# Cached keys fetched page by page, score products at full height, and grouped products in a one-layer decoder kernel

## The chip, the cores and the metric

The kernel runs on one core of a Trainium2 chip. The metric is device time in microseconds (us) of one execution; the median of several runs is compared. Within a core five engines work from in-order queues of their own: PE (matrix products), DVE (vector), ACT (scalar functions and copies), POOL (which here mostly issues gathers) and SP (which here issues loads). An instruction that waits holds up everything behind it in its queue.

## The reference

One decoder layer is applied with the same weights to 512 prompt tokens and to 8 sample rows of 4 tokens each. The parts that the change touches belong to the sample rows' sparse attention and to the norms:

```python
def dsa_sample(q, k_new, v_new, qi, ki_new, wi, ck, cv, cki, page_table):
    ...
    ki_past = cki[page_table].reshape(DB, PAST_LEN, IDX_DIM)
    ki_all = jnp.concatenate([ki_past, ki_new], axis=1)
    sc = index_scores(qi, wi, ki_all)
    ...
    _, idx = lax.top_k(sc, topk)
    ...
    k_sel = jnp.where(is_new, k_new[bi, new_idx], ck[phys, off])
    v_sel = jnp.where(is_new, v_new[bi, new_idx], cv[phys, off])
    return sparse_attend(q, k_sel, v_sel, valid)
```

Each sample row has 2048 cached tokens in 16 pages of 128 tokens, found through a page table; index keys, keys and values each lie in a paged cache. The best 256 of 2052 tokens by index score take part in a softmax attention. The prompt has the same attention over its own 512 tokens. Then come a gMLP mix, the output projection, an attention to a 256-token memory, a product-key expert layer of 16384 experts with the best 16 of each of 8 heads, and norms (mean of squares over 1024 features) before each of these.

## The kernel before

**Main stream.** Every large projection is the function `mm3`: a float32 product is made of three products of rounded halves (lines 249, 250 and 251). `wtile` loads a weight tile of 512 KB by SP (line 225), ACT casts it to the upper half (line 213) and DVE subtracts to get the lower half (line 217, called the split below). The raw tile and both halves have two buffers each, so the load of tile k waits for the split of tile k-2, and the cast of tile k waits for the products of tile k-2. I count the main products in order of program: w_in takes numbers 1 to 912, the memory keys and values (wKV, tiles K1 to K8) 913 to 1104, then for the first half of the prompt eight tiles of the output projection (wO1 to wO8) and four of the memory queries (wMQ1 to wMQ4) up to 1392; behind 1392 comes the second half (h1), with its own eight wO tiles, later the experts.

**Work beside it.** Generators run between the main products:

- The mask search for the prompt: a search by bits for each token's threshold score, in which ACT counts (line 695, two activations a bit, 32 bits) and DVE decides (lines 698, 705, 692). Lines 706 to 727 finish it, and the prompt's attention (lines 854 to 890: scores 854, softmax 860 to 867, transposes 880, values 886) follows.
- The sample rows: index scores (`sample_scores`, products at line 1359, a batch for each of 8 rows), the select (`sample_select`, 32 bits on DVE, line 1413 first in each bit, lines 1426 to 1453 behind the last), scores of the cached keys (`sample_keys`, line 1496, evacuated at line 1500), and the attention proper (`sample_attend`: lines 1562 and 1535 spread the selection, 1545 and 1546 turn the weights, 1553 is the product with the values, a round for each row, 1601 to 1638 close it).
- The norms: `squares4` sums squares on PE with four small products (line 147) in four column groups.

**What sets the order.** The program is recorded through a scheduler that plans all engines on a timeline of its own and writes each engine's queue in that order; pools of few buffers and the generators' yields shape it. So an edit can move instructions that it does not touch.

**Fetches.** Pages of index keys (32 KB) are fetched by SP (line 1317 reads a page number, line 1319 issues the transfer), 8 behind each weight load. Cached keys and values are gathered by POOL (line 1276), four gathers of 128 pieces for each sample row, into a ring of three buffers (`RING`) which keys use first and values after them.

Of the kernel before, what the change touches and what calls it, by code (L numbers as in the profile page):

```python
# [10 lines left out]
I32 = mybir.dt.int32  # L11
U32 = mybir.dt.uint32
AF = mybir.ActivationFunctionType
ALU = mybir.AluOpType
AX = mybir.AxisListType
# [3 lines left out]
P = 128  # L19
NP = 512  # L20
NS = 32
NT = NP + NS
KT = 8
# [28 lines left out]
class Kernel:  # L52
# [84 lines left out]


    def squares4(self, room, x, kt, st, w):
        sq = self.t(room, [P, w], tag="nsqs", bufs=4)  # L140
        self.nc.scalar.square(sq, x)
        self.sq4 = [sq] if kt % 4 == 0 else self.sq4 + [sq]
        if kt % 4 == 3:
            n = w // len(st)
            for i, ps in enumerate(st):
                for c, q in enumerate(self.sq4):
                    self.nc.tensor.matmul(ps[c * NS : c * NS + NS, :n], self.ones[:, :NS], q[:, i * n : i * n + n],
                                          start=kt == 3, stop=kt == KT - 1, skip_group_check=True)

# [69 lines left out]
    def wtile(self, pool, src, kt=KT, n=P):  # L219

        more = pool is self.pw and self.gp is not None and self.RX
        if more:
            self.raws = (self.raws + 1) % (2 + self.RX)
        raw = self.t(self.gp, [P, kt, n], tag="wraw", bufs=self.RX) if more and self.raws > 1 else self.t(pool, [P, kt, n], tag="wraw", bufs=2)
        load = self.nc.sync.dma_start(raw, src)  # L225
        self.loads += 1
        if self.todo and self.loads > 2:
            self.index_rows(load)
        hi = self.t(pool, [P, kt, n], F32R, tag="whi", bufs=2)
        lo = self.t(pool, [P, kt, n], F32R, tag="wlo", bufs=2)  # L230
        self.split(hi, lo, raw)
        return hi, lo
# [399 lines left out]
    def masks(self, pool, room, qiT, kiT, wi_n, mb):  # L632
        nc = self.nc
        scs = []
        for b in range(1, 4):
# [4 lines left out]
            for h in range(8):  # L640
                if h % 2 == 0:

                    pair = [self.pst("pb") for _ in range(2)]
                    for o, ps in zip((0, 64), pair):
                        nc.tensor.matmul(ps[:, :L], qiT[o : o + 64, h // 2, ts], kiT[o : o + 64, :L], start=True, stop=True)
                ps = pair[h % 2]
# [198 lines left out]
    def attend(self, pw, qT, kT, v_n, mb):  # L845
# [24 lines left out]
        def values(b, r, sms):  # L870
# [11 lines left out]
            if r % 2:  # L882

                for s in range(b + 1):
                    for g in range(2):
                        nc.tensor.matmul(yb[g * 64 : g * 64 + 64, (r - 1) * P : (r + 1) * P], v_n[:, s, g * 64 : g * 64 + 64],
                                         keep[g][:, s, :, :], start=s == 0, stop=s == b, skip_group_check=True)
            if r == 3:
# [372 lines left out]
    def fetch_kv(self, s2):  # L1261
        n = len(self.kv)
        if n < 16:
            kv = self.t(s2, [P, 2048], tag="kv", bufs=self.RING)
            kv = kv.rearrange("p (m x) -> p m x", m=4)
            for m in range(4):
                self.gather(kv[:, m, :], self.I["cV" if n >= 8 else "cK"], self.s_ix[:, n * 4 + m : n * 4 + m + 1])
            self.kv.append(kv)

    RING = 3  # L1270
# [8 lines left out]
    def pages(self, s1, s2):  # L1279
# [3 lines left out]
        for r in range(0, P, 32):  # L1283
            nc.gpsimd.iota(pid[r : r + 32], [[0, 1]], base=0, channel_multiplier=1, allow_small_or_imprecise_dtypes=True)
        pt_i = self.t(s1, [P, P], I32)
        nc.gpsimd.dma_start(pt_i, I["page_table"].rearrange("b n -> (b n)").partition_broadcast(P))
        pf = self.t(s1, [P, P])
        nc.vector.tensor_copy(pf, pt_i)
        self.s_ix = self.t(s1, [P, 64], I32)
        tmp = self.t(s1, [P, 64])  # L1290
        for u in range(4):
            r = slice(u * 32, u * 32 + 32)

            nc.vector.tensor_scalar(tmp[r, :32].rearrange("p (b c f) -> p b c f", c=2, f=2),
                                    pf[r].rearrange("p (b c v r f) -> p v r b c f", c=2, v=2, r=2, f=2)[:, u % 2, u // 2],
                                    32.0, pid[r], ALU.mult, ALU.add)
            nc.vector.tensor_scalar(tmp[r, 32:], pf[r].rearrange("p (n u) -> p u n", u=4)[:, u], 32.0, pid[r], ALU.mult, ALU.add)
        nc.vector.tensor_copy(self.s_ix, tmp)

        self.kv, self.rows, self.indexed, self.keyed = [], [], False, False  # L1300
        for b in range(8):
            if b % 2 == 0:
                kx = self.t(s1, [P, 4, 512], tag="S8", bufs=2) if b < 4 else self.t(s2, [P, 2048], tag="kv", bufs=self.RING).rearrange("p (b x) -> p b x", b=4)
            self.rows.append(kx[:, b % 2 * 2 : b % 2 * 2 + 2, :].rearrange("p b (m x) -> p (b m) x", x=P))
        self.todo, self.loads = [(pt_i, b, m) for b in range(8) for m in range(8)], 0
        for _ in range(self.RING - 2):
            self.fetch_kv(s2)


    def index_rows(self, behind):  # L1310
        nc = self.nc
        src = self.I["cI"].rearrange("(n d) x -> n d x", d=64)
        with self.tc.issue_after(getattr(behind, "ins", behind)):
            for pt_i, b, m in self.todo[: self.PAGES]:
                for c in range(2):
                    n = b * 16 + 2 * m + c
                    page = nc.values_load(pt_i[:1, n : n + 1], engines=[mybir.EngineType.SP], min_val=0, max_val=src.shape[0] - 1,
                                          skip_runtime_bounds_check_because="a page table holds pages of the pool")
                    nc.sync.dma_start(self.rows[b][c * 64 : c * 64 + 64, m, :], src[bass.ds(page, 1)].rearrange("n d x -> (n d) x"))
        self.todo = self.todo[self.PAGES :]  # L1320

    PAGES = 4


    def sample_scores(self, s1, s2):
# [26 lines left out]
        for b in range(8):  # L1352
            kx = self.rows[b]
            while any(x[1] == b for x in self.todo):
                yield 1.0
# [101 lines left out]
    def sample_keys(self, s1, s2):  # L1457
# [8 lines left out]

        qs = self.t(s2, [P, 4, 8, 16])
        self.s_room = Room(qs.rearrange("p e b q -> p (e b q)"))
        ps = self.pst("pb")
        for e in range(4):  # L1470
            perm = self.t(s1, [P, P], tag="qst", bufs=2)
            nc.vector.tensor_copy(perm.rearrange("p (u g d) -> p u g d", u=4, g=2),
                                  self.ident.rearrange("p (g e d) -> p e g d", g=2, e=4)[:, e].unsqueeze(1).to_broadcast([P, 4, 2, 16]))
            nc.tensor.matmul(ps[:, e * P : e * P + P], perm, self.s_q.rearrange("p r t -> p (r t)"), start=True, stop=True)
        for e in range(4):
            nc.scalar.activation(qs[:, e].rearrange("p b (r t) -> p r b t", r=4), ps[:, e * P : e * P + P].rearrange("p (r b t) -> p r b t", r=4, b=8),
                                 AF.Copy, scale=0.125)

        own = self.t(s2, [P, 4])
        nc.vector.tensor_reduce(own, self.ident.rearrange("p (r c d) -> p c r d", r=2, d=16), AX.XY, ALU.add)  # L1480
        yield 1.0
# [4 lines left out]
        for b in range(8):  # L1486
            q4 = self.t(s2, [P, 4, 64], tag="q4", bufs=2)
            nc.vector.tensor_tensor(q4.rearrange("p e (c q) -> p e c q", c=4), qs[:, :, b].unsqueeze(2).to_broadcast([P, 4, 4, 16]),
                                    own.unsqueeze(1).unsqueeze(3).to_broadcast([P, 4, 4, 16]), ALU.mult)

            pair = [self.pst("pb") for _ in range(2)]
            for e in range(4):
                for f in range(2):
                    for o, ps in zip((0, 64), pair):
                        for c in range(2):
                            nc.tensor.matmul(ps[c * 64 : c * 64 + 64, f * P : f * P + P], q4[o : o + 64, e],
                                             self.kv[b][o : o + 64, 2 * c + f, e * P : e * P + P], start=e == 0 and f == 0, stop=e == 3,
                                             skip_group_check=True, tile_position=(o, c * 64))
            for r, ps in enumerate(pair):
                nc.scalar.copy(self.s_S[b].rearrange("p (m r f x) -> p r f m x", m=4, r=2, f=2)[:, r],  # L1500
                               ps[:, : 2 * P].rearrange("p (f m x) -> p f m x", f=2, m=4))
            self.fetch_kv(s2)
            yield 4.0 * self.SK
        self.keyed = True

    SK = 1.0

    def sample_attend(self, s2, s1):
# [40 lines left out]
        def values(b, A):  # L1549
            po = self.pst("pb")  # L1550
            for m in range(4):
                for c in range(4):
                    nc.tensor.matmul(po[c * NS : c * NS + NS, :P], A[:, m, c, :], self.kv[8 + b][:, c, m * P : m * P + P],  # L1553
                                     start=m == 0, stop=m == 3)
            nc.scalar.copy(part(b), po[:, :P])
            self.fetch_kv(s2)
# [314 lines left out]
```

## Time and profile before

| | |
|---|---|
| median of 3 runs | 1797.67 us (1795.82 to 1801.38) |
| the profiled execution, its own time | 1793.41 us |
| its span in the trace | 1791.7 us |
| PE busy | 1675.7 us, 94% |
| DVE busy | 1482.9 us, 83% |
| ACT busy | 863.2 us, 48% |
| POOL busy | 503.6 us, 28% |
| main products (lines 249 to 251), busy | 2515 us of overlapping records, 2544 of each line |
| DMA | 460.36 MB, mean 257 GB/s |

Busy time is what the records of an engine cover; matrix products overlap in PE's pipeline, so the sum over a line can be larger than the engine's busy time. The profiled execution lies 4.3 us below the median of the runs.

### The profile page before, as it was taken

How to read it: one execution, taken by the hardware profiler on the slowest of the kernel's cores; microseconds unless marked ns; L12 is line 12 of the kernel's file. 1: busy time of each engine (PE TensorE's matmuls, PEld its weight loads, DVE VectorE, ACT ScalarE, POOL GpSimd, SP SyncE). 2: the span in 40 equal slices, each digit the busy share in tenths (PEclk: the TensorE clock that was granted, in tenths of full speed). 3: DMA queues.
4: the chain of work that ended last, by engine and by line, in shares of the span. 5: the costliest groups of instructions: out<-in, count | busy, mean ns of one | idle time of the engine just before them, and what ended most of it. 6: DMA issues, size and time to landing. Idle time of an engine off the chain costs nothing. (4 is left out here: it accounts for less than half of the span.)

```text
span 1791.7 us, 30106 instructions
## 1 busy us (share of the span) xinstructions
PE 1675.7 (94%) x10494; PEld 1476.6 (82%) x10494; DVE 1482.9 (83%) x3654; ACT 863.2 (48%) x1584; POOL 503.6 (28%) x437
## 2 busy tenths in 40 slices
PE   7999889989996999799999999999999999999995
PEld 5879757778875889789899998888788888888884
DVE  4586899755759999998999887799898888878897
ACT  4355765764543434674675575233343333333333
POOL 3000123120000054223224222334333534345343
PEclk9999769989998999999999999999999999999997
DMA  5423425445752599789779789799998999999986
GB/s 179 128 83 98 126 85 199 140 166 170 238 172 90 169 345 329 267 316 334 256 269 322 242 306 316 267 353 333 360 356 300 375 357 328 349 334 324 358 305 231
DMA packets 195207, 460.36 MB, mean 257 GB/s; under 512 B 17976, under 2 KB 98616, under 8 KB 193648
## 3 DMA queue, kind: packets, MB, share of 16 engines
q1 hardware_dynamic: 132928, 241.63, 39.7%
q0 software_dynamic: 53072, 207.71, 32.5%
q10 hardware_dynamic: 9056, 9.11, 1.6%
q8 instruction: 82, 1.34, 0.3%
q14 instruction: 69, 0.57, 0.1%
HBM read 416.11 MB, written 42.05 MB: 256 GB/s over the span
## 5 line engine op out<-in xcount | busy, mean ns | idle before, releaser
L251 PE MATMUL t<-t,t 128*128 128x384 f32 (+3 forms) x2544 | 867.9, 346 | 12.5 <-DVE t L217 12.2
L250 PE MATMUL t<-t,t 128*128 128x384 f32 (+3 forms) x2544 | 867.6, 343 | 0.0
L249 PE MATMUL t<-t,t 128*128 128x384 f32 (+3 forms) x2544 | 779.9, 346 | 17.6 <-ACT t L213 15.1
L213 ACT CAST t<-t 128x1024 fp32r<-128x1024 f32 (+4 forms) x512 | 418.2, 841 | 716.8 <-PE t L250 475.8
L217 DVE TENSOR_TENSOR t<-t,t 128x1024 fp32r<-128x1024 f32 (+4 forms) x512 | 488.6, 965 | 140.0 <-ACT t L213 136.3
L251 PEld LDWEIGHTS t<-t,t 128*128 128x128 f32 x2544 | 485.0, 191 | 66.4 <-DVE t L217 15.7
L249 PEld LDWEIGHTS t<-t,t 128*128 128x128 f32 x2544 | 485.0, 191 | 61.2 <-ACT t L213 20.3
L250 PEld LDWEIGHTS t<-t,t 128*128 128x128 f32 x2544 | 485.4, 191 | 38.4 <-issue 5.7
L1276 POOL DMA_INDIRECT t<-in_u,t x160 | 201.7, 1260 | 499.0 <-DVE t L1736 305.0
L1276 POOL DMA_INDIRECT t<-in_v,t x160 | 215.5, 1347 | 298.0 <-DVE t L1741 233.9
L1741 DVE SCALAR_TENSOR_TENSOR t<-t,t,t 128x1024 f32<-128x1024 f32 x160 | 204.9, 1281 | 4.5 <-DMA t<-in_v,t 3.6
L1736 DVE SCALAR_TENSOR_TENSOR t<-t,t 128x1024 f32<-128x1024 f32 x160 | 193.8, 1219 | 8.7 <-DMA t<-in_u,t 8.6
L1081 ACT ACTIVATE t<-t 128x512 f32<-128x512 f32 x96 | 96.6, 1148 | 19.3 <-DMA wd<-t 18.5
L1276 POOL DMA_INDIRECT t<-in_cK,t x32 | 32.3, 1009 | 212.1 <-PE t L1359 146.5
L1217 DVE TENSOR_TENSOR t<-t,t 128x352 f32<-128x352 f32 x128 | 66.6, 521 | 6.2 <-DMA t<-wd 4.0
L1097 ACT ACTIVATE t<-t 128x384 f32<-128x384 f32 x128 | 62.3, 487 | 11.8 <-PE t L251 9.2
L1071 ACT ACTIVATE t<-t,t 128x128 f16<-128x128 f16 x192 | 58.2, 395 | 10.1 <-DVE t L1067 7.4
L1078 PE MATMUL t<-t,t 128*128 128x128 f16 x384 | 51.8, 221 | 9.4 <-ACT t L1081 8.8
L1276 POOL DMA_INDIRECT t<-in_cV,t x32 | 34.2, 1069 | 72.0 <-PE t L1553 45.1
L695 ACT ACTIVATE t<-t,t 128x384 f32<-128x384 f32 x64 | 42.7, 666 | 24.4 <-DVE t L692 20.3
L1079 PE MATMUL t<-t,t 128*128 128x128 f16 x384 | 49.7, 221 | 0.4 <-DVE t L1073 0.3
L1079 PEld LDWEIGHTS <-t 128*128 128x128 f16 x384 | 36.7, 98 | 10.6 <-issue 10.1
(400 smaller groups left out, 1471.2 us busy)
## 6 DMA issues: line engine op xcount, KB each, us to landing
t<-in_uT SPq DMA_DIRECT2D x128, 512.0 KB, 5.8
t<-in_v SPq DMA_DIRECT2D x128, 512.0 KB, 6.2
wd<-t POOLq DMA_DIRECT2D x11, 2048.0 KB, 9.2
t<-wd SPq DMA_DIRECT2D x32, 704.0 KB, 7.9
gd<-t SPq DMA_DIRECT2D x56, 192.0 KB, 5.3
t<-gd SPq DMA_DIRECT2D x56, 192.0 KB, 7.6
t<-in_wA SPq DMA_DIRECT2D x19, 512.0 KB, 4.0
t<-in_wO SPq DMA_DIRECT2D x16, 512.0 KB, 4.0
```

Of the source, the lines that this page charges most:

```text
L213: self.nc.scalar.copy(hi, x)
L217: self.pin_v = self.nc.vector.tensor_tensor(lo, x, hi, ALU.subtract)
L249: mm(out, ah, bh, start=first, stop=False)
L250: mm(out, ah, bl, start=False, stop=False)
L251: self.pin = mm(out, al, bh, start=False, stop=last)
L1079: nc.tensor.matmul(o, oj[:, x, :], ol[:, x, :], start=False, stop=True)
L1081: nc.scalar.activation(wb[:, :, t : t + 4].rearrange("p i t -> p t i"), ps.rearrange("p (t i) -> p t i", t=4), AF.Copy, scale=1.0 / 2048.0)
L1097: nc.scalar.activation(G, ps, AF.Gelu_apprx_tanh)
L1217: nc.vector.tensor_tensor(q(w)[:, : 4 * NB - 1], self.wp[:, :, i % 4, :], q(G)[:, : 4 * NB - 1], ALU.mult)
L1276: self.nc.gpsimd.indirect_dma_start(out=out, out_offset=None, in_=src, in_offset=bass.IndirectOffsetOnAxis(ap=ix, axis=0))
L1736: nc.vector.scalar_tensor_tensor(r, r, 1.0, hf, ALU.mult, ALU.mult, accum_out=a[:, k : k + 1])
L1741: nc.vector.scalar_tensor_tensor(acc, r, a[:, k : k + 1], acc, ALU.mult, ALU.add)
```

## The change

**Keys by page.** The 32 POOL gathers of cached keys go. Each of the 128 pages (64 KB) is now one SP transfer, taken from the list `todo` that index pages use too; `fetch_pages` issues 6 behind each weight load and, where pages lack, in the loop of `sample_keys`. Before it was 4 entries of two pages each. The source is read in the pattern page, 4 (e), 32 (d), 128.

**Scores at full height.** The 512 products of line 1496 (64 rows by 64 columns, 64x128 out) become 32 products (128 rows by 32 columns, 32x512 out, line 1492 of the changed kernel), four for each sample row; the query is permuted by one product in place of four.

**Groups.** `together` emits the last member of a group first and pins the others behind it: for the norms' squares, the prompt's index scores and the prompt's value products.

```diff
+    def together(self, products):
+        first = products[-1]()
+        with self.tc.issue_after(getattr(first, "ins", first)):
+            for p in products[:-1]:
+                p()
...
-                for c, q in enumerate(self.sq4):
-                    self.nc.tensor.matmul(ps[c * NS : c * NS + NS, :n], self.ones[:, :NS], q[:, i * n : i * n + n],
-                                          start=kt == 3, stop=kt == KT - 1, skip_group_check=True)
+                self.together([lambda c=c, q=q: self.nc.tensor.matmul(ps[c * NS : c * NS + NS, :n], self.ones[:, :NS], q[:, i * n : i * n + n],
+                                                                      start=kt == 3, stop=kt == KT - 1, skip_group_check=True)
+                               for c, q in enumerate(self.sq4)])
...
-        load = self.nc.sync.dma_start(raw, src)
+        self.pin_s = self.nc.sync.dma_start(raw, src)
         self.loads += 1
-        if self.todo and self.loads > 2:
-            self.index_rows(load)
+        if self.loads > 2:
+            self.fetch_pages()
...
-            for m in range(4):
-                self.gather(kv[:, m, :], self.I["cV" if n >= 8 else "cK"], self.s_ix[:, n * 4 + m : n * 4 + m + 1])
+            if n < 8:
+                src = self.I["cK"].rearrange("(n d) (e x) -> n e d x", d=32, e=4)
+                self.todo += [(kv[:, m * P : m * P + P], src, 16 * n + m) for m in range(16)]
+            else:
+                for m in range(4):
+                    self.gather(kv[:, m * 512 : m * 512 + 512], self.I["cV"], self.s_ix[:, (n - 8) * 4 + m : (n - 8) * 4 + m + 1])
             self.kv.append(kv)
+
+
+    def fetch_pages(self):
+        nc = self.nc
+        with self.tc.issue_after(getattr(self.pin_s, "ins", self.pin_s)):
+            for out, src, n in self.todo[: self.PAGES]:
+                page = nc.values_load(self.s_pt[:1, n : n + 1], engines=[mybir.EngineType.SP], min_val=0, max_val=src.shape[0] - 1,
+                                      skip_runtime_bounds_check_because="a page table holds pages of the pool")
+                x = src[bass.ds(page, 1)]
+                nc.sync.dma_start(out, x.rearrange("n d x -> (n d) x") if len(x.shape) == 3 else x[0])
+        self.todo = self.todo[self.PAGES :]
+
+    PAGES = 6
...
-            for e in range(4):
-                for f in range(2):
-                    for o, ps in zip((0, 64), pair):
-                        for c in range(2):
-                            nc.tensor.matmul(ps[c * 64 : c * 64 + 64, f * P : f * P + P], q4[o : o + 64, e],
-                                             self.kv[b][o : o + 64, 2 * c + f, e * P : e * P + P], start=e == 0 and f == 0, stop=e == 3,
-                                             skip_group_check=True, tile_position=(o, c * 64))
-            for r, ps in enumerate(pair):
-                nc.scalar.copy(self.s_S[b].rearrange("p (m r f x) -> p r f m x", m=4, r=2, f=2)[:, r],
-                               ps[:, : 2 * P].rearrange("p (f m x) -> p f m x", f=2, m=4))
+
+            while len(self.todo) > 16 * (min(len(self.kv), 8) - b - 1):
+                self.fetch_pages()
+                yield self.SP
+            ps = self.pst("pb")
+            for c in range(4):
+                nc.tensor.matmul(ps[c * NS : c * NS + NS, :], q3[:, b], self.kv[b][:, c * 512 : c * 512 + 512],
+                                 start=True, stop=True)
+            nc.scalar.copy(self.s_S[b].rearrange("p (m u x) -> p u m x", m=4, u=4), ps.rearrange("p (u m x) -> p u m x", u=4, m=4))
             self.fetch_kv(s2)
```

The order of the queues moves with it. Three places matter below. In the changed kernel lines are shifted: the cast of line 213 is line 220 there, the search's line 695 is 702, the split of line 217 is 224, the select's line 1413 is 1418, and the values' line 1553 is 1547.

**ACT, at the cast of tile K7.** Before, the cast of K7 (the last row here) stands behind the prompt's softmax steps of lines 864 and 867, and the mask search is long over:

```order
L867 ACTIVATE t_3671<-t_3671,t_3678 128x384
L213 CAST t_3880<-t_3878 128x1024
L1500 COPY t_2890<-t_3742 128x2x4x32
L1500 COPY t_2890<-t_3743 128x2x4x32
L763 COPY t_150<-t_3784 128x2x128
L213 CAST t_3973<-t_3971 128x1024
```

In the changed kernel (the first cast here is K6's, the last K7's) the search's last seven bits, fourteen activations of line 702, stand between the two casts:

```order
L220 CAST t_3331<-t_3305 128x1024
L220 CAST t_144<-t_149 128x256 x4
L702 ACTIVATE t_158,t_945<-t_158,t_942 128x384
L702 ACTIVATE t_158,t_945<-t_158,t_942 128x512
...
L871 ACTIVATE t_3065,t_3070<-t_3065,t_3068 128x384
L871 ACTIVATE t_3075,t_3080<-t_3075,t_3078 128x384
...
L874 ACTIVATE t_3168<-t_3168,t_3175 128x384
L220 CAST t_3438<-t_3412 128x1024
```

In the first listing t_3880 is the cast of K7 and t_3973 that of K8. What moved: the seven bits and the steps that finish the search come ahead of K7's cast; on DVE, K7's split stands behind line 727's successors in the same way.

**SP, from tile wO1 on.** Before, the loads of wO stand one behind the other:

```order
L225 DMA t_3971<-in_wKV 128x1024
L225 DMA t_4083<-in_wO 128x1024
L225 DMA t_4137<-in_wO 128x1024
L225 DMA t_4226<-in_wO 128x1024
L225 DMA t_4269<-in_wO 128x1024
```

In the changed kernel pages of cached keys (three rows each) stand between them; here wO2, its six pages, and wO3:

```order
L232 DMA t_3734<-in_wO 128x1024
L1285 TENSOR_LOAD t_123
L1288 ISA
L1288 DMA t_3260<-in_cK 128x1x128
...
L232 DMA t_3853<-in_wO 128x1024
```

Between wKV5 and wO1 there are now 32 pages of cached keys (and two last index pages), and behind the loads of wO1 to wO8 and wMQ1 to wMQ4 stand 8, 6, 6, 12, 6, 6, 6, 18, 12, 6, 6 and 4 pages: all 128 lie in this stretch, 92 of them between the load of wO1 and that of wMQ4.

**DVE and PE, at the end of the select.** In the changed kernel the split of the second wO tile of h1 (the first row) stands ahead of the 28th of the select's 32 bits:

```order
L224 TENSOR_TENSOR t_5517<-t_5514,t_5516 128x1024
L1417 SCALAR_TENSOR_TENSOR t_3546<-t_3544,t_3545 128x1
L794 RECIPROCAL t_5040<-t_5037 128x2
L788 TENSOR_SCALAR t_5095<-t_5095 128x2
L787 TENSOR_REDUCE t_5182<-t_5179 128x2
L1418 SCALAR_TENSOR_TENSOR t_3531,t_3548<-t_3530,t_3546,t_58 128x544
```

Before, the same split (t_5311) stood between two late rounds of the attention itself, with the select over long ago:

```order
L217 TENSOR_TENSOR t_5311<-t_5308,t_5310 128x1024
L781 TENSOR_SCALAR t_5117<-t_5117 128x2
L1537 ISA t_2890,t_4300<-t_4816,t_2890 128x512
L1537 ISA t_4300 128x1
L1522 TENSOR_SCALAR t_4821<-t_4300 128x1
```

On PE, line 1562 stood at main product 1246, four of the eight value rounds of line 1553 between products 1303 and 1392 and four behind; now all of these stand behind product 1392, with nothing of the main stream between them:

```order
L258 MATMUL t_4928<-t_144,t_4925 128x256
L1492 MATMUL t_4953<-t_4344,t_2598 32x512
L785 MATMUL t_5031<-t_142,t_4655 128x256
L785 MATMUL t_5092<-t_142,t_4655 128x256 x2
L800 MATMUL t_4976<-t_60,t_3654 128x128 x4
L785 MATMUL t_5179<-t_142,t_4655 128x256 x2
L1556 LDWEIGHTS t_4986
L1556 MATMUL t_4989<-t_3527,t_4986 128x32
```

Here line 258 is main product 1392 and line 1556 is the former line 1562. Besides, the 34 separate runs of the norms' squares on PE become 10, of which the 23 runs behind product 1392 become 6, and the 24 runs of the prompt's index scores stay 24. Two of the eight batches of index scores (line 1359) move from ahead of product 912 to behind it, the 24 index pages that SP issued in one block ahead of product 816 are spread, and the scores of the cached keys move from products 912 to 1080 to products 1056 to 1392.

## Rows read from the trace of the kernel before

**Rows 1.** Stretch: its length, PE, PEld, DVE, ACT, POOL busy, clock, DMA share, GB/s.

```profile
560.00:1790.00 1230.00, 1170.62 (x6491) 1055.42 (x6491) 1092.92 (x2299) 560.55 (x896) 424.43 (x332) 0.98 0.87 308
```

**Rows 2.** Timeline of PE, pause at product 912: start, us, engine, line, idle before.

```profile
190.23 0.48 PE L854 MATMUL t<-t,t 64*128 64x128 f32 x2
...
192.82 2.00 PE L1359 MATMUL t<-t,t 128*128 128x64 f32 x16
...
210.10 5.02 PE L1496 MATMUL t<-t,t 64*64 64x128 f32 x88
...
238.65 0.47 PE L880 MATMUL t<-t,t 128*128 128x128 f32 x1 [4.39 <-ACT t L1500]
...
251.19 0.58 PE L249 MATMUL t<-t,t 128*128 128x256 f32 x1
```

**Rows 3.** Timeline of ACT: a late cast, two bits of the search, K6's cast.

```profile
172.69 1.04 ACT L213 CAST t<-t 128x1024 fp32r<-128x1024 f32 x1 [6.71 <-DMA t<-in_wA]
...
219.21 0.61 ACT L695 ACTIVATE t<-t,t 128x384 f32<-128x384 f32 x1 [0.68 <-DVE t L692]
...
221.45 0.61 ACT L695 ACTIVATE t<-t,t 128x384 f32<-128x384 f32 x1 [0.42 <-DVE t L692]
...
280.53 1.35 ACT L213 CAST t<-t 128x256 fp32r<-128x256 f32 x2
```

**Rows 4.** Timeline of DVE: the search's finish, two bits of the select, its end.

```profile
245.91 0.16 DVE L615 TENSOR_SCALAR t<-t 128x2 uint32<-128x2 uint32 x1
...
264.42 0.43 DVE L727 TENSOR_SCALAR t<-t 128x512 f32<-128x512 f32 x1
...
305.62 0.79 DVE L1413 SCALAR_TENSOR_TENSOR t<-t,t,t 128x544 f32<-128x544 f32 x1
...
307.98 0.79 DVE L1413 SCALAR_TENSOR_TENSOR t<-t,t,t 128x544 f32<-128x544 f32 x1
...
312.46 0.78 DVE L1413 SCALAR_TENSOR_TENSOR t<-t,t,t 128x544 f32<-128x544 f32 x1
...
329.65 0.18 DVE L1453 TENSOR_SCALAR t<-t 128x32 bf16<-128x32 f32 x1
```

**Rows 5.** Timeline of SP's queue: eight index pages between loads; loads without pages.

```profile
51.47 0.53 SPq L225 DMA_DIRECT2D t<-in_wA  x1
52.51 7.21 SPq L1319 DMA_DIRECT2D t<-in_cI  x8
59.82 0.54 SPq L225 DMA_DIRECT2D t<-in_wA  x1
...
289.93 38.40 SPq L225 DMA_DIRECT2D t<-in_wO  x8
```

**Rows 6.** DMA: us from issue to landing; queue of the pages, share of 16 engines.

```profile
t<-in_wO SPq DMA_DIRECT2D x16, 512.0 KB, 4.0
t<-in_cV,t POOLq DMA_INDIRECT x32, 4.6
q10 hardware_dynamic: 9056, 9.11, 1.6%
```

**Rows 7.** Timeline of PE: selection spread, last value round, its close, main stream again.

```profile
332.77 0.19 PE L1562 MATMUL t<-t,t 128*128 128x32 bf16 x1
...
384.39 1.08 PE L1553 MATMUL t<-t,t 128*32 128x128 f32 x32 [0.73 <-ACT t L1546]
...
391.03 1.59 PE L1635 MATMUL t<-t,t 128*128 128x32 f32 x8
...
403.10 0.48 PE L249 MATMUL t<-t,t 128*128 128x288 f32 x1
```

**Rows 8.** Timeline of POOL: one of the four value gathers of a row.

```profile
364.87 0.95 POOL L1276 DMA_INDIRECT t<-in_cV,t  x1 [0.30 <-issue]
```

**Rows 9.** Timeline of PE: norm squares, runs of four and of two.

```profile
413.24 0.68 PE L147 MATMUL t<-t,t 128*32 128x288 f32 x4
...
417.27 0.67 PE L147 MATMUL t<-t,t 128*32 128x288 f32 x2
```

More of the change, by code (lines that the diff above doesn't have):

```diff
@@ L643, in masks @@
                     pair = [self.pst("pb") for _ in range(2)]
-                    for o, ps in zip((0, 64), pair):
-                        nc.tensor.matmul(ps[:, :L], qiT[o : o + 64, h // 2, ts], kiT[o : o + 64, :L], start=True, stop=True)
+                    self.together([lambda o=o, ps=ps: nc.tensor.matmul(ps[:, :L], qiT[o : o + 64, h // 2, ts], kiT[o : o + 64, :L], start=True, stop=True)
+                                   for o, ps in zip((0, 64), pair)])
                 ps = pair[h % 2]
@@ L884, in values @@
                 for s in range(b + 1):
-                    for g in range(2):
-                        nc.tensor.matmul(yb[g * 64 : g * 64 + 64, (r - 1) * P : (r + 1) * P], v_n[:, s, g * 64 : g * 64 + 64],
-                                         keep[g][:, s, :, :], start=s == 0, stop=s == b, skip_group_check=True)
+                    self.together([lambda g=g: nc.tensor.matmul(yb[g * 64 : g * 64 + 64, (r - 1) * P : (r + 1) * P], v_n[:, s, g * 64 : g * 64 + 64],
+                                                                keep[g][:, s, :, :], start=s == 0, stop=s == b, skip_group_check=True)
+                                   for g in range(2)])
             if r == 3:
@@ L1284, in pages @@
             nc.gpsimd.iota(pid[r : r + 32], [[0, 1]], base=0, channel_multiplier=1, allow_small_or_imprecise_dtypes=True)
-        pt_i = self.t(s1, [P, P], I32)
+        pt_i = self.s_pt = self.t(s1, [P, P], I32)
         nc.gpsimd.dma_start(pt_i, I["page_table"].rearrange("b n -> (b n)").partition_broadcast(P))
@@ L1288, in pages @@
         nc.vector.tensor_copy(pf, pt_i)
-        self.s_ix = self.t(s1, [P, 64], I32)
-        tmp = self.t(s1, [P, 64])
+        self.s_ix = self.t(s1, [P, 32], I32)
+        tmp = self.t(s1, [P, 32])
         for u in range(4):
             r = slice(u * 32, u * 32 + 32)
[L1294 to L1297, printed above, removed]
+            nc.vector.tensor_scalar(tmp[r], pf[r].rearrange("p (n u) -> p u n", u=4)[:, u], 32.0, pid[r], ALU.mult, ALU.add)
         nc.vector.tensor_copy(self.s_ix, tmp)
@@ L1304, in pages @@
             self.rows.append(kx[:, b % 2 * 2 : b % 2 * 2 + 2, :].rearrange("p b (m x) -> p (b m) x", x=P))
-        self.todo, self.loads = [(pt_i, b, m) for b in range(8) for m in range(8)], 0
+        src = I["cI"].rearrange("(n d) x -> n d x", d=64)
+        self.todo, self.loads = [(self.rows[b][c * 64 : c * 64 + 64, m, :], src, 16 * b + 2 * m + c) for b in range(8) for m in range(8) for c in range(2)], 0
         for _ in range(self.RING - 2):
             self.fetch_kv(s2)
[L1310 to L1314, printed above, removed]
-                for c in range(2):
[L1316 to L1322, printed above, removed]
     def sample_scores(self, s1, s2):
@@ L1353, in sample_scores @@
             kx = self.rows[b]
-            while any(x[1] == b for x in self.todo):
+            while len(self.todo) > 16 * (7 - b + len(self.kv)):
                 yield 1.0
@@ L1465, in sample_keys @@
                 nc.vector.tensor_scalar(qb[r, :, g, q], self.s_q[r, q].rearrange("p (b t) -> p b t", t=4), 0.125, None, ALU.mult)
-        qs = self.t(s2, [P, 4, 8, 16])
-        self.s_room = Room(qs.rearrange("p e b q -> p (e b q)"))
+        perm = self.t(s1, [P, P], tag="qst", bufs=2)
+        nc.vector.tensor_copy(perm.rearrange("p (e g d) -> p e g d", e=4, g=2), self.ident.rearrange("p (g e d) -> p e g d", g=2, e=4))
         ps = self.pst("pb")
-        for e in range(4):
[L1471 to L1480, printed above, removed]
+        nc.tensor.matmul(ps[:, :256], perm, qb.rearrange("p b g r t -> p (b g r t)"), start=True, stop=True)
+        room = self.t(s2, [P, 512])
+        q3 = room[:, :256].rearrange("p (b q) -> p b q", b=8)
+        nc.scalar.copy(room[:, :256], ps[:, :256])
+        self.s_room = Room(room)
         yield 1.0
@@ L1486, in sample_keys @@
         for b in range(8):
[L1487 to L1492, printed above, removed]
-                for f in range(2):
-                    for o, ps in zip((0, 64), pair):
-                        for c in range(2):
-                            nc.tensor.matmul(ps[c * 64 : c * 64 + 64, f * P : f * P + P], q4[o : o + 64, e],
-                                             self.kv[b][o : o + 64, 2 * c + f, e * P : e * P + P], start=e == 0 and f == 0, stop=e == 3,
-                                             skip_group_check=True, tile_position=(o, c * 64))
-            for r, ps in enumerate(pair):
-                nc.scalar.copy(self.s_S[b].rearrange("p (m r f x) -> p r f m x", m=4, r=2, f=2)[:, r],
-                               ps[:, : 2 * P].rearrange("p (f m x) -> p f m x", f=2, m=4))
+            while len(self.todo) > 16 * (min(len(self.kv), 8) - b - 1):
[6 more added lines that the diff above has]
+            nc.scalar.copy(self.s_S[b].rearrange("p (m u x) -> p u m x", m=4, u=4), ps.rearrange("p (u m x) -> p u m x", u=4, m=4))
             self.fetch_kv(s2)
@@ L1504, in sample_keys @@
         self.keyed = True
+    SP = 4.0
     SK = 1.0
@@ L1552, in values @@
                 for c in range(4):
[L1553 removed]
+                    nc.tensor.matmul(po[c * NS : c * NS + NS, :P], A[:, m, c, :], self.kv[8 + b][:, c * 512 + m * P : c * 512 + m * P + P],
                                      start=m == 0, stop=m == 3)
```

1 line of the change is left out of this document (removed).

## The prediction

> **What bounds the kernel now.** I read the busy time by stretches first. From 560 us on PE is busy 1170.6 of 1230 us [rows 1]: that part is a stream of main products, and whatever makes it start later or earlier moves the end by as much. The change touches the part before, so I looked there for the places where the main stream stops, with the timeline of PE. The two long ones are at product 912, from 190.2 to 251.2 us [rows 2], and at product 1392, where the stream goes on at 403.1 us [rows 7]. The first holds 28.5 us from the start of the score products of line 1496 at 210.1 to the product at 238.65 that ACT's evacuations let through [rows 2]. The second is the end of the sample rows' attention. In the queues I then followed what each of these waits for: the order of the changed program says what stands ahead, and the trace says how long each takes.
>
> **The gains.** (1) The block of line 1496 leaves the pause at product 912, which becomes 61.0 - 28.5 = 32.5 us. (2) The cast that came 6.7 us late behind a page block [rows 3] comes in time, and two batches of index scores at 2.0 us each [rows 2] move behind product 912, so the pause begins at 190.2 - 6.7 - 4.0 = 179.5 and ends at 212 instead of 251. (3) The norms' squares: a run takes PE 0.67 us with two products and 0.68 with four [rows 9], so 23 runs that become 6 save 17 x 0.675 = 11.5 us in a stream that PE limits; bounds 8 (a third lies in gaps) and 13. (4) Off the path: 32 POOL gathers of keys, at the 1.25 us of those of values [rows 8], the fewer evacuations, and the fewer runs of value products (hidden under the waits on SP below; 7 runs, so about 5 us if those go). The index scores keep their 24 runs: that edit changes nothing.
>
> **Where the gain is lost: tile K7.** From the end of the pause to K6's cast it took 280.5 - 251.2 = 29.3 us before [rows 2, 3]; from 212 this gives 241.5, and the cast is over at 243. Now seven bits of the mask search stand between this cast and K7's on ACT. A bit takes 221.45 - 219.21 = 2.24 us [rows 3], a ping-pong of ACT and DVE, so 15.7 us. The search's finish took 264.4 - 245.9 = 18.5 us on DVE [rows 4] and K7's cast waits for softmax steps that stand behind it, its split for the finish itself. Sum: 243 + 15.7 + 18.5 + 1.2 for cast and split = 278 us. The lower bound is 272 (before, bits of the select lay within those 18.5 us, a third of them perhaps), the upper 288. So K7's split is just 10 us earlier than before, though the pause ended 39 us earlier. In the raw buffers the load of wO1 waits for this split, so SP stands at wO1 until 278.
>
> **Where more is lost: SP.** Behind wO1 SP has 92 pages of cached keys before it comes to wMQ4's load. A load and eight pages took 59.82 - 51.47 = 8.35 us [rows 5], and eight pages alone 7.21, so a page takes about 0.96 us and a load about 0.66. The eight wO loads without pages went at 38.4 / 8 = 4.8 us each [rows 5], as the products used them up; a tile with six pages needs 6 x 0.96 + 0.66 = 6.4. The 92 pages and 11 loads need 88.3 + 7.3 = 95.6 us, so wMQ4 is loaded at 278 + 95.6 = 374. The trace shows no page of 128 pieces; the nearest row is the 64-piece page, and a 512 KB load costs 0.53 to issue [rows 5] against 0.47 for a page, so size hardly counts: I take 0.96. Bounds: 0 if pages lie in time that SP would wait anyway, and 1.4 if the issue of 128 pieces takes twice as long, which adds 41 us.
>
> **What comes behind.** Tile wMQ4 lands 4.0 us later (the time of wO's loads [rows 6]), cast and split take 2.3, and only then, at 380, may the second wO tile of h1 be loaded; its split ends at 387. On DVE the 28th to 32nd bit of the select stand behind that split. A bit takes 307.98 - 305.62 = 2.36 us [rows 4], five take 11.8. The steps from the 32nd bit to the end took 329.65 - 312.46 = 17.2 us among other work [rows 4]; alone I set 9, bounds 7 and 17. The selection is ready at 387 + 11.8 + 9 = 408, and line 1562, which stood at 332.8 [rows 7], runs then, 75 us later than before. All of it lies behind product 1392, with PE idle but for the attention itself. For the first round of values I set 7 us. The ring of three buffers holds the first three rows; the other five are gathered as the rounds free them, four gathers of 0.95 + 0.30 us [rows 8] each, so 5 x 5.0 = 25 us on POOL, and the last lands 4.6 us behind [rows 6]: the last round starts 7 + 25 + 4.6 = 36.6 us behind line 1562 (before it was 51.6 with the main stream between [rows 7], my upper bound). The close up to line 1635 took 391.0 - 384.4 = 6.6 us [rows 7]; its second half, cast and split of the result I set at 5. The stream goes on at 408 + 36.6 + 11.6 = 456 us against 403.1: 53 us later.
>
> **Sum.** +53 - 11.5 = +41.5 us, so the profiled execution's own 1793.4 becomes 1834.9. It lies 4.3 us below the median of the runs shown, so I put the median at 1839.
>
> **Does a page use all DMA engines?** The queue of the index pages took 1.6% of 16 engines' span for 9056 packets and 9.11 MB [rows 6], which is 459 us of engine time: 0.051 us for each packet, or 19.9 KB per us on one engine. If a page spread over 16 engines, this would stay far below SP's pace. [...]
>
> **Rivals.**
> *Pages hidden* (0.20). SP's pages lie in its waits, and the select is bound by itself: it starts some 10 us behind K7's split (288), 32 bits take 75.5, the end 9, line 1562 at 372.5, the stream again at 372.5 + 48.2 = 420.7, +17.6 - 11.5 = +6: about 1804. For it: the select is long, and its bits between the splits nearly fill the time themselves. Against: SP has no wait left once a tile costs 6.4 us.
> *Four engines* (0.10). A page is carried by four of the 16 engines, 32 pieces on each. By bytes that is 16.4 / 19.9 = 0.82 us, and a weight load 32.8 / 19.9 = 1.65: a tile with six pages 6.6 us, hardly over SP's 6.4. By packets it is 32 x 0.051 = 1.63 us a page, 92 x 1.63 + 11 x 1.65 = 168 us in place of 95.6, so up to 72 us more: 1840 to 1911. Most of the packets there were small, so I hold the price by bytes for the nearer.
> *Faster: K7 is not held* (0.14). The seven bits find the search further on than I think, K7's cast follows K6's by 7 us as it did, and the pages are hidden: K7's split at 251, the select from 261, line 1562 at 346, the stream again at 394, -9 - 11.5: about 1777. The point is line 1562 at 361: earlier than that is faster by over 0.3%, which needs K7's split before 266 and hidden pages together.
> *Same* (0.09). Line 1562 between 361 and 372, the grouping's gain and part of the first pause's paying for the exposed attention.
>
> **How the numbers follow.** A measurement of this kernel tells about 0.3%, 5.4 us, from no change. My forecast (0.47) is 1839; with K7's split at 272 to 288, the value chain up to 15 us longer and the select's end between its bounds it runs from 1822 to 1866. Pages hidden is 1803 to 1822, and it is slower, as are four engines. So slower is 0.47 + 0.20 + 0.10 = 0.77, same 0.09, faster 0.14. The range from 1793 to 1866 holds the forecast, hidden pages, the same and half of four engines: 0.81.
>
> **What will show it.** The pause at product 912 should shrink to about 33 us and end near 212. K7's split should come near 278, directly behind the search's finish. Pages of cached keys should go at 0.96 us each, with SP without gaps from wO1 to wMQ4. The main stream should stand at product 1392 for some 70 us, with line 1562 near 408 and five value gathers back to back behind it. Runs of line 147 should be of four, 0.68 us. I am wrong if K7's split comes before 266, if SP waits among the pages, if line 1562 comes near 372, or if the selection is ready when product 1392 is reached.

## The result and the profile after

The changed kernel takes 1900.3 us (median of 4 runs, 1897.7 to 1903.0) against 1797.6 us: the ratio is 1.0569, with an interval from 1.0546 to 1.0591. It is slower, as forecast, but by 103 us and not by 41, and outside the range.

The profiled execution has a span of 1901.3 us, 109.6 more than before. The timeline of PE in the changed kernel (start, us, engine, line, idle before) shows the two stops of the main stream; the products of lines 249 to 251 are lines 256 to 258 there:

```profile
180.40 0.50 PE L135 MATMUL t<-t,t 128*128 128x1 f32 x4
...
214.28 0.58 PE L256 MATMUL t<-t,t 128*128 128x256 f32 x1
...
466.74 0.21 PE L1556 MATMUL t<-t,t 128*128 128x32 bf16 x1 [19.23 <-DVE t L1458]
...
509.53 1.07 PE L1547 MATMUL t<-t,t 128*32 128x128 f32 x28
...
518.29 0.85 PE L256 MATMUL t<-t,t 128*128 128x288 f32 x2 [0.56 <-ACT t L220]
```

The stop at product 912 lasts from 180.4 to 214.3 us, 33.9 in place of 61.0 [rows 2]; I had forecast 179.5 to 212. But the stream goes on behind product 1392 at 518.3 us and not at 403.1 [rows 7], 115.2 later. From there to the end it takes 1901.3 - 518.3 = 1383.0 us against 1791.7 - 403.1 = 1388.6. So 115.2 - 5.6 = 109.6: all of the loss lies ahead of 518 us.

SP's queue in the changed kernel, from the first page of cached keys to wMQ4's load:

```profile
225.02 14.94 SPq L1288 DMA_DIRECT2D t<-in_cK  x10
240.05 0.38 SPq L232 DMA_DIRECT2D t<-in_wKV  x1
241.12 8.39 SPq L1288 DMA_DIRECT2D t<-in_cK  x6
249.62 0.38 SPq L232 DMA_DIRECT2D t<-in_wKV  x1
250.76 8.39 SPq L1288 DMA_DIRECT2D t<-in_cK  x6
259.24 0.38 SPq L232 DMA_DIRECT2D t<-in_wKV  x1
260.31 14.97 SPq L1288 DMA_DIRECT2D t<-in_cK  x10
279.90 0.35 SPq L232 DMA_DIRECT2D t<-in_wO  x1
281.13 11.59 SPq L1288 DMA_DIRECT2D t<-in_cK  x8
...
429.13 0.38 SPq L232 DMA_DIRECT2D t<-in_wMQ  x1
```

Set this beside [rows 5]. Eight pages took 7.21 us there and 11.59 here, so a page goes at about 1.57 us (11.59 less the last issue of 0.59, over seven) and not at 0.96. wO1 is loaded at 279.9, where I had 278. From there to wMQ4's load it is 149.2 us and not the 95.6 of my sum, 54 us more, and SP waits for other engines for only 2.4 us of it.

That wO1 waits for K7's split, and K7 for the mask search, is in ACT's and DVE's timelines. On ACT these are a group of casts whose first is K6's, the seven bits behind it at 2.23 us each (the first and the last are shown), and K7's cast; on DVE the end of the search's finish (line 734, the former 727) and K7's split, which ends at 279.9.

```profile
244.66 2.27 ACT L220 CAST t<-t 128x1024 fp32r<-128x1024 f32 x5 [4.75 <-DMA t<-in_wKV]
246.84 0.61 ACT L702 ACTIVATE t<-t,t 128x384 f32<-128x384 f32 x1
...
260.23 0.61 ACT L702 ACTIVATE t<-t,t 128x384 f32<-128x384 f32 x1 [0.68 <-DVE t L699]
...
277.56 1.05 ACT L220 CAST t<-t 128x1024 fp32r<-128x1024 f32 x1
```

```profile
275.19 0.43 DVE L734 TENSOR_SCALAR t<-t 128x512 f32<-128x512 f32 x1
278.65 1.23 DVE L224 TENSOR_TENSOR t<-t,t 128x1024 fp32r<-128x1024 f32 x1 [0.54 <-ACT t L220]
...
300.18 0.78 DVE L1418 SCALAR_TENSOR_TENSOR t<-t,t,t 128x544 f32<-128x544 f32 x1
...
448.16 0.77 DVE L1418 SCALAR_TENSOR_TENSOR t<-t,t,t 128x544 f32<-128x544 f32 x1
...
457.69 0.79 DVE L1418 SCALAR_TENSOR_TENSOR t<-t,t,t 128x544 f32<-128x544 f32 x1
...
466.51 0.17 DVE L1458 TENSOR_SCALAR t<-t 128x32 bf16<-128x32 f32 x1
```

The last four rows on DVE are the select: its first, 28th and 32nd bit and its end. It starts at 300.2 us, where it stood at 206.1 before (the first execution of line 1413 in the trace before), and ends at 466.5 where the end was at 329.7 [rows 4].

### The profile page after: what moved, and what is told of

Read it like the earlier page. It is cut to its first block, busy times and chain, and to the rows that moved or that the text cites. A ratio compares the mean times of both kernels' runs of the same rounds, so it can differ in the third digit from the quotient of the medians.

```text
span 1901.3 us, 29703 instructions
## 1 busy us (share of the span) xinstructions
PE 1676.3 (88%) x10038; PEld 1462.1 (77%) x10040; DVE 1488.0 (78%) x3638; ACT 862.0 (45%) x1573; POOL 465.3 (24%) x405
## 3 DMA queue, kind: packets, MB, share of 16 engines
q10 hardware_dynamic: 9056, 9.11, 1.5%
## 4 chain that ended last, share of the span: by engine, by line
PE 59%; DVE 15%; issue 7%; DMA 7%; ACT 4%; SPq 4%; POOL 2%; another core or an unknown queue 0%; ACTq 0%; POOLq 0%; DVEq 0%
PE t L256 17%; PE t L258 17%; PE t L257 17%; DVE t L224 3%; SPq L1285 2%; POOL t L1299 2%; SPq L1288 2%; DMA t<-in_u,t 2%; DVE t L1730 2%; DMA t<-in_uT 1%; PE t L651 1%; ACT t L220 1%; DVE t L940 1%; DMA wd<-t 1%; ACT t L702 1%
## 5 line engine op out<-in xcount | busy, mean ns | idle before, releaser
L220 ACT CAST t<-t 128x1024 fp32r<-128x1024 f32 (+5 forms) x512 | 418.4, 842 | 754.5 <-PE t L257 505.4
L224 DVE TENSOR_TENSOR t<-t,t 128x1024 fp32r<-128x1024 f32 (+5 forms) x512 | 487.1, 963 | 176.8 <-ACT t L220 153.6
L1492 PE MATMUL t<-t,t 128*32 128x512 f32 x64 | 29.0, 722 | 28.5 <-DMA t<-in_cK 28.0
```

The costliest lines, as they stand in the source:

```text
L220: self.nc.scalar.copy(hi, x)
L224: self.pin_v = self.nc.vector.tensor_tensor(lo, x, hi, ALU.subtract)
```

## The experiments

Twelve kernels ran, each beside the kernel before on the same chip (1796.3 to 1796.8 us).

**The pattern of a page.** *k16* reads the same bytes in 128 rows:

```diff
-                src = self.I["cK"].rearrange("(n d) (e x) -> n e d x", d=32, e=4)
+                src = self.I["cK"].rearrange("(n d) (e x) -> n (d e) x", d=32, e=4)
...
-        nc.vector.tensor_copy(perm.rearrange("p (e g d) -> p e g d", e=4, g=2), self.ident.rearrange("p (g e d) -> p e g d", g=2, e=4))
+        nc.vector.tensor_copy(perm.rearrange("p (g d e) -> p g d e", e=4, g=2), self.ident.rearrange("p (g e d) -> p g d e", g=2, e=4))
```

> The changed kernel, but a page of cached keys is read in its natural order of 128 rows of 512 bytes (pattern 128 x 128) instead of 4 x 32 x 128; the query's permutation follows, so the same values come out. The order of SP's queue stays as it was. Theory (the pattern with a slowest dimension of 4 makes a page dear to issue): a page goes back from 1.50 us to the 0.96 us that I had taken from the index pages, the 92 pages between the loads of wO1 and wMQ4 take 50 us less, line 1556 and the end follow, about 1850 us (1840 to 1860). Rival (128 pieces in place of 64 are what costs): a page stays at 1.4 to 1.5 us and the time at 1895 to 1905.

It took 1835.5 us (1.0203 of before, 1.0178 to 1.0228), 65 us less than the changed kernel, with the same order of loads and pages on SP. Its queue at the same place:

```profile
273.19 0.34 SPq L232 DMA_DIRECT2D t<-in_wO  x1
274.49 6.13 SPq L1288 DMA_DIRECT2D t<-in_cK  x8
280.72 0.38 SPq L232 DMA_DIRECT2D t<-in_wO  x1
281.60 4.49 SPq L1288 DMA_DIRECT2D t<-in_cK  x6
```

Eight pages take 6.13 us, 0.83 each. The theory holds, and the time lies 5 us below the range that it gave because a page went to 0.83 us and not only to 0.96: a page of 128 pieces is even cheaper than an index page of 64.

**Which patterns are dear.** *k16_steps* and *k8* keep steps as in the changed kernel, with 16 or 8 in place of 4 as the slowest dimension (here 8), and the permutation to match (not shown):

```diff
-                src = self.I["cK"].rearrange("(n d) (e x) -> n e d x", d=32, e=4)
+                src = self.I["cK"].rearrange("(n d) (e x) -> n (d e) x", d=32, e=4).rearrange("n (h l) x -> n l h x", l=8)
```

> As k16 (6 pages behind a load), but the page's rows in the pattern 16 x 8 x 128: steps as in the changed kernel, with a slowest dimension of 16. Theory (the size of the slowest dimension sets a page's price on SP): 0.8 us a page as in k16, time 1825 to 1845 us. Rival (a pattern of three dimensions is dear whatever its sizes): 1.5 us a page, 1890 to 1905 us.

> The same with the pattern 8 x 16 x 128. Theory (slowest dimension, price falling with it): between the two, 0.95 to 1.2 us a page, time 1840 to 1870 us. Rival (only divisors of 16 or nothing): 1.5 us and about 1900. Rival of three dimensions: 1.5 us too, and then k16_steps the same.

They took 1853.2 us (1.0311, 1.0269 to 1.0353) and 1900.2 us (1.0573, 1.0530 to 1.0615), two runs each. The view by tile gives the issue of a page, in ns (least, median, most). The changed kernel, k16, k16_steps and k8 in turn:

```profile
L1288 SPq DMA_DIRECT2D t<-in_cK x128: 3/591/657, 225.0 to 435.0; - x128
```

```profile
L1288 SPq DMA_DIRECT2D t<-in_cK x128: 332/333/808, 223.8 to 363.7; - x128
```

```profile
L1288 SPq DMA_DIRECT2D t<-in_cK x128: 529/540/838, 223.7 to 383.4; - x128
```

```profile
L1288 SPq DMA_DIRECT2D t<-in_cK x128: 3/653/716, 225.7 to 441.6; - x128
```

Besides, the read of the page number ahead of each issue changes. The view of that line has index pages and keys together: a median of 448 and 461 ns in the changed kernel and in k8, 268 and 267 in k16 and k16_steps:

```profile
L1285 SPq TENSOR_LOAD <-t x256: 262/448/1289, 16.9 to 434.0; - x128
```

```profile
L1285 SPq TENSOR_LOAD <-t x256: 260/268/1516, 17.0 to 363.2; - x128
```

These medians mix two kinds of read. One directly behind a page of keys took 0.73 us in the changed kernel and in k8, and 0.27 in the other two; one behind an index page 0.27 in all four.

So the size of the slowest dimension counts, but not in proportion: 8 is as dear as 4 (1.63 us a page, from five pages in 7.15 us less the last issue of 0.65, over four, against 1.57). The three dimensions of k16_steps cost 0.2 us of issue beside k16's two, so it came 8 us above the range that I expected; and with 4 and 8 the read of the page number behind a page takes longer too. My expectation for k8 was wrong; its first rival came near in price and time (1.5 us and about 1900), though 8 too divides 16.

What a page moved can be read from the queue of SP's transfers in the kernel before, the changed kernel, k8 and k16 in turn (packets, MB, share of 16 engines):

```profile
q1 hardware_dynamic: 132928, 241.63, 39.7%
```

```profile
q1 hardware_dynamic: 149824, 250.02, 39.4%
```

```profile
q1 hardware_dynamic: 150336, 250.02, 39.3%
```

```profile
q1 hardware_dynamic: 151360, 250.03, 40.8%
```

128 pages of 128 pieces are 16384 packets. Beyond these the queue grew by 512, 1024 and 2048, in k16_steps by 2048 as well: 4, 8, 16 and 16 packets for each page. In the trace of the changed kernel they are of 4 bytes: one page (its packets move from 287.2 to 288.4 us) is 128 packets of 512 bytes and 4 of 4, and one weight load (280.9 to 283.2) 128 of 4096 and 16 of 4. The records do not say which engine carried a packet. The load's 16 are as many as the engines over which the view takes its share, so I take one small packet for each engine that had a part: by this estimate from the counts a page of the changed kernel used 4 engines and one of k8 used 8. Neither number of engines set the pace: in the trace of the changed kernel a piece of 512 bytes took 27 ns (median), so by my estimate 32 of them on one engine need 0.86 us of the 1.57, and 16 of them 0.43 of k8's 1.63.

**Without SP's issue.** *static_k* has k16's pattern and issues one transfer for each row's 16 pages, so 8 in place of 128; it leaves out the page table and reads 16 neighbouring pages:

```diff
             for out, src, n in self.todo[: self.PAGES]:
+                if src.shape[1] == P:
+                    if n % 16 == 0:
+                        row = self.kv[n // 16].rearrange("p (m x) -> p m x", x=P)
+                        nc.sync.dma_start(row, src[n : n + 16].rearrange("m p x -> p m x"))
+                    continue
```

> As k16, but of each sample row's 16 pages only one transfer of 1 MB is issued, from 16 neighbouring pages without the page table (so the keys are those of other pages); all the rest of the program is left in place. Theory (SP's issue of pages bounds the stage from wO1 to wMQ4, and behind it the select): that stage takes 50 to 65 us as before the change, the select is then the bound, line 1556 comes near 373 and the time at 1800 to 1815 us. Rival (the bytes or the landing of the keys bound it, not the issue): within 10 us of k16. Second rival (the order of the queues costs nothing by itself): 1775 to 1795, faster than the kernel before.

It took 1832.9 us (1.0207, 1.0190 to 1.0224), as k16, though product 1392 is passed at 353 us. My expectation of 1800 to 1815 was wrong: what bounds here is the select. It starts at 290.4 us, its 32nd bit at 394.9, and PE waits 42 us for its end:

```profile
403.93 0.18 PE L1561 MATMUL t<-t,t 128*128 128x32 bf16 x1 [42.17 <-DVE t L1463]
```

104.5 us for 31 bits are 3.4 us each, not 2.36 [rows 4]: while the main stream runs, DVE's splits and the prompt's steps lie between the bits. The trace before had said so: from the first bit at 206.1 to the 32nd at 312.5 it is 106.4 us. So once a page costs 0.83 us, the pages cost little (2.5 us between the medians of k16 and static_k, 12 between their two profiled executions); the late start of the select costs more. That start had to be explained.

**The number of pages behind a load.** *before_p6* changes one number in the kernel before, from 4 entries of two index pages to 3:

```diff
-    PAGES = 4
+    PAGES = 3
```

> The kernel before with one number changed: 6 index pages behind each weight load in place of 8. Theory (the smaller count brings the last index pages late, so the scheduler writes the select and all of the sample rows' attention behind tile K7 and product 1392, and this is the larger part of the loss): the order shows it, the select starts near 290 us instead of 206, the main stream goes on behind product 1392 near 450 instead of 403, and the time is 1835 to 1850 us. Rival (the new fetch of keys moves the select, not the count): 1795 to 1805 us.

It took 1860.8 us (1.0341, 1.0307 to 1.0375): 64 us more from this number alone. The order agrees with the theory. In the kernel before, seven of the eight batches of index scores stand at product 816 or ahead of it and the select starts at product 912; with 6 pages a load three batches stand at 912 and later (912, 960, 1043), the select starts at product 1104, and line 1562 and all value rounds stand behind product 1392, as in the changed kernel. In its trace, the last index pages on SP, and the first and the last bit on DVE:

```profile
224.56 1.51 SPq L1319 DMA_DIRECT2D t<-in_cI  x2
```

```profile
294.12 0.78 DVE L1413 SCALAR_TENSOR_TENSOR t<-t,t,t 128x544 f32<-128x544 f32 x1
...
394.17 0.79 DVE L1413 SCALAR_TENSOR_TENSOR t<-t,t,t 128x544 f32<-128x544 f32 x1
```

The last index pages go behind 224.6 us; the kernel before had them out at 177. *p8* and *k16_p8* go the other way: the changed kernel and k16 with 8 pages behind a load.

```diff
-    PAGES = 6
+    PAGES = 8
```

> The changed kernel with 8 pages behind each load in place of 6, the pattern of 4 x 32 x 128 kept. Theory of the count: the select starts near 200 us and most of the 103 us are gone; pages at 1.50 us still hold loads of wKV and wO back by 30 us or so: 1790 to 1830 us. Rival (the pages' price alone is the cause): 1880 to 1905 us.

> As the last, but with pages read as 128 rows, so at 0.8 us each. Theory (count and pattern together are the whole loss): faster than the kernel before, 1770 to 1790 us. Rival (the exposed attention or the missing overlap stays): 1800 to 1835 us.

p8 took 1860.1 us (1.0366, 1.0340 to 1.0392), k16_p8 1804.1 us (1.0036, 1.0003 to 1.0070). Both start the select at 204 and 201 us again. The four kernels make a table:

| | pattern 4 x 32 x 128 | 128 rows |
|---|---|---|
| 6 pages a load | 1900.3 (the change) | 1835.5 (k16) |
| 8 pages a load | 1860.1 (p8) | 1804.1 (k16_p8) |

The pattern costs 65 or 56 us, the count 40 or 31. Both of my expectations were too low: p8's 1790 to 1830 allowed some 30 us for the pages at 1.50 us each, and k16_p8 was to be faster than the kernel before; it came into its rival's range. Its queue shows what is left:

```profile
284.79 5.42 SPq L232 DMA_DIRECT2D t<-in_wO  x2
294.93 14.04 SPq L1288 DMA_DIRECT2D t<-in_cK  x16
309.06 0.46 SPq L232 DMA_DIRECT2D t<-in_wO  x1
312.38 13.29 SPq L1288 DMA_DIRECT2D t<-in_cK  x16
325.77 14.84 SPq L232 DMA_DIRECT2D t<-in_wO  x5
```

The last two rows' pages go in blocks of 16, and loads of wO stand behind them: the main stream stops for 8 us at product 1152 and for 13 at 1176, and goes on behind product 1392 at 420.

*k16_p16* tries the other end, 16 pages a load.

> As the last with 16 pages behind each load: the order then has the select near product 484 and only one round of values behind product 1392. Theory (the earlier the pages, the less attention is exposed): 1755 to 1785 us. Rival (blocks of 16 pages hold the loads of w_in back and PE waits there for more than is won): 1790 us and more.

It took 1819.7 us (1.0128, 1.0108 to 1.0148). The rival holds: product 912 is reached at 243 us instead of 181, since blocks of 16 pages hold back the loads of w_in.

**The grouping.** *no_group* emits the members one by one in the changed kernel, *group_only* puts `together` alone into the kernel before:

```diff
     def together(self, products):
-        first = products[-1]()
-        with self.tc.issue_after(getattr(first, "ins", first)):
-            for p in products[:-1]:
-                p()
+        for p in products:
+            p()
```

> The changed kernel without the grouping (the members of a group are emitted one by one). Theory (17 runs of squares fewer save about 0.67 us each, or somewhat less since the stretch behind the attention was only 5.6 us shorter): 5 to 12 us longer than the changed kernel, 1905 to 1912 us. Rival (gaps in the stream hide the runs): 1898 to 1903.

> The kernel before with the grouping alone; keys gathered and scored as before. Theory: 5 to 12 us faster than the kernel before, 1786 to 1792 us. Rival (the pinned order makes waits of its own in the crowded stage before 560 us, or gaps hide the runs): 1795 to 1805 us.

group_only took 1784.4 us (0.9929, 0.9912 to 0.9946): 12 us faster, and the fastest kernel here. It has all three groupings, while my term of 11.5 us was for the norms alone; between the two profiled executions the stretch behind product 1392 is 7.4 us shorter (1381.2 us in place of 1388.6). no_group took 1899.1 us, no different from the changed kernel: the rival's number, but not for the rival's reason. In its trace the stretch from the end of the stop at product 1392 is 12 us longer (1395.1 us in place of 1383.0), but that stop ends 13 us earlier (505.5). So the grouping saves as much there, and the schedule that comes with it loses it ahead.

**More index pages a load, with the grouping.** Since group_only beats both kernels, *group_p10* and *group_p12* vary its count (10 and 12 index pages a load).

> The kernel before with the grouping and 10 index pages behind a load in place of 8. The order then has the select near product 800 in place of 912 and one value round behind product 1392 in place of three. Theory (the exposed attention is what the count sets): faster than the grouping alone (1784), 1760 to 1782 us. Rival (blocks of ten pages hold loads of w_in back by as much): 1782 to 1795 us.

> The same with 12 index pages behind a load; no value round stands behind product 1392. Theory: 1755 to 1780 us. Rival (the loads of w_in are held back by more than the attention gives): 1785 to 1800 us, as 16 pages a load did in the kernel with paged keys.

They took 1788.1 us (0.9952, 0.9934 to 0.9970) and 1809.9 us (1.0066, 1.0040 to 1.0092). Product 912 is reached at 194 and 208 us in place of 190, and what the attention gives back behind product 1392 does not pay for it. Both expectations of a gain were wrong: ten pages came into the rival's range and are no better than eight, twelve are slower than even the rival said. Eight stays.

## Why the prediction was wrong

**Right, with its size.** The stop at product 912 (33.9 us, forecast 32.5). K7's chain: seven bits between the casts, split at 278.7 us, forecast 278; to the microsecond that is luck, since the bits began at 246.8 and not at 243, and from their end to K7's cast it took 15.1 us and not 18.5. wO1's load at 279.9. SP without gaps from there on, but for 2.4 us of waits. The select's last bits behind the split of h1's second tile, and from the 32nd bit to the end 8.8 us, forecast 9. From line 1556 to the last value round 42.8 us, forecast 36.6; from there to the main stream 8.8, forecast 11.6. The groups: 12 us by group_only's medians, 7.4 by its trace behind product 1392, forecast 11.5 for the norms; their runs became six of eight products (0.69 us), where I had written of runs of four.

**The term that was mis-sized: "size hardly counts: I take 0.96".** I took a page's price from index pages, which have a plain pattern of rows, and gave no thought to the pattern as a price on SP. It was 1.57 us; 92 pages and 11 loads took 149.2 us and not 95.6. Those 54 us, and 6 in the value chain, are the difference between 456 and 518 for the end of the stop, but for a net 3 us. With 1.57 us in place of 0.96 the same sum gives 1839 + 56 = 1895. k16 shows that the pattern is the cause and not the 128 pieces: with it undone the kernel takes 1835.5. I had named an upper bound of 1.4 us, which gives 1880, and left it out of the range; but it too was below the measured price.

**The rival that came nearest** was "four engines", at 1840 to 1911, but not by its mechanism. No row of the kernel before shows its four engines; what the trace of the changed kernel shows are the four small packets of each page on q1, which fit them. But it had each engine's share of the pieces as the bound; then k8, with half the share on each by its eight packets, would have been much cheaper than the changed kernel, and it is not (1900.2 us against 1900.3). Its price per packet was also read from the wrong row: q10 [rows 6] is not the pages' queue, for it has the same 9056 packets in the changed kernel, while q1 has the pages. What the runs show is that the issue and the next read on SP take longer: 0.59 and 0.73 us in the changed kernel and 0.65 and 0.73 in k8, against 0.33 and 0.27 in k16 and 0.54 and 0.27 in k16_steps. So the read behind a page is longer in the two patterns with 4 and 8 small packets and not in those with 16; a price that falls from 4 to 8 the runs do not show (1.57 us a page and 1.63).

**What I did not see at all** is why the order was what it was. I read the late select and the exposed value rounds off the order and priced them, but took them as given by K7 and the keys' pages. The runs say that one number is enough: 6 index pages behind a load in place of 8 costs 64 us in the kernel before, with nothing of the new fetch in it, and going back to 8 gives 40 us in the changed kernel. And "pages hidden" at 1804 was wrong, since it let the select's bits run at 2.36 us, the distance of two undisturbed bits; static_k, which comes near that case, took 1833. k16 with 0.83 us a page took 1835.5 and k16_steps with 1.04 (eight pages in 7.80 us) 1853.2, so at my 0.96 it would have been about 1846, an estimate by a line between the two: near 1839, though no run shows it.

**Open.** What on SP takes the longer time with a slowest dimension of 4 or 8, and why 8 is not cheaper than 4; and why the grouping's schedule loses in the changed kernel what the grouping saves. And whether a fetch by page can beat the gather with a schedule that spreads the last pages: k16_p8 is 0.4% behind the kernel before, 20 us behind group_only.

## What to carry to other kernels

Price a transfer's issue from a row with the same access pattern, not with the same size, and where there is none, carry the bound into the range. In a kernel that a scheduler orders, when a chain has moved as a whole, look for what feeds it first: a count of fetches per load can move it as well as the edit beside it, and changing that number alone in the kernel before is a cheap test. A change of several parts should be run part by part: here one part by itself made the kernel before 12 us faster, and the whole hid it.

## What was not expected of the hardware

The issue of a page of 64 KB on SP took 0.33 us as 128 rows, 0.54 us as 16 x 8 rows, 0.65 as 8 x 16 and 0.59 as 4 x 32, and an index page of 64 rows and 32 KB 0.47 us, more than the 128 rows. With 4 and 8 as the slowest dimension the read of a page number directly behind such a page took 0.73 us in place of 0.27. A page moved 4, 8, 16 and 16 packets besides its pieces with 4, 8, 16 and 128 as the slowest dimension.
